# The Units stage of a dilated-attention layer: VectorE, ScalarE and GpSimd ordered by hand beside TensorE, with rope, mixes, weight pairs and loads cut into steps over several slots

## The chip, the cores and the metric

The kernel runs on one core of one Trainium2 chip. The metric is the device time of one execution in microseconds (us), the median of several runs; lower is better. A core has engines with a queue of instructions each: TensorE (PE, with its weight loads as PEld), VectorE (DVE), ScalarE (ACT), GpSimd (POOL) and SyncE (SP), which here only issues DMAs. An engine goes through its queue in order; an instruction whose data isn't there holds up those behind it.

## The reference

Two pre-norm residual layers on 2048 tokens of width 1024: the first with gated linear attention, the second with dilated sliding-window attention in three groups of heads (window and dilation 128/1, 512/4, 2048/16; six heads of width 128 in each); each layer also has a small attention into a memory, a SiLU gate and an output projection. The change touches the second layer's mixer:

```
def dilated_mixer(h, w_in):
    for g, (window, dil) in enumerate(DIL_GROUPS):
        qkv = (h @ w_in[:, base:base + 3 * MIXER_WIDTH]).reshape(B, T, 3, DIL_HEADS, DIL_HEAD_DIM)
        q = partial_rope(qkv[:, :, 0], pos)          # rotates 32 of the 128 columns
        k = partial_rope(qkv[:, :, 1], pos)
        o, lse = dilated_group(q, k, qkv[:, :, 2], window, dil)
    wts = jax.nn.softmax(jnp.stack(lses, axis=0), axis=0)
    o = jnp.einsum('gbth,gbthd->bthd', wts, jnp.stack(outs, axis=0).astype(jnp.float32))
```

So the three groups' outputs of one head number are mixed with weights from the groups' log-sum-exps: a mix needs all three.

## The kernel before, in words

Products are made in three 16-bit matmuls (`mm3`, L180 to L182: high by high, high by low, low by high), so each operand exists as a high and a low half. The Units stage takes up the second layer's heads: 18 heads, in triples of groups 2, 1, 0, eight slots each, 144 slots s. In slot s, PE does the scores of step s - 10 (`att_scores`), the values of step s - 13 (`att_pv`), and one projection `proj_t` of 24 matmuls (q on even slots, k on odd ones, 512 tokens each). PE's order is written out by hand (`manual_schedule` at L1157); DVE, ACT, POOL and SP get theirs from a scheduler, which places the instructions by when it reckons them ready.

What the other engines do for one slot:

- scores: DVE adds the mask and takes the maximum (L1234, into pm and mx), makes the bias st (L1238); ACT takes the exponential with its row sum (L1243); `split_P` cuts pm into the high half (L173, ACT) and the low half (L174, POOL), and SP transposes both by DMA (L175, ph to pt). The values' matmuls three slots later read pt. Every second step DVE copies the output bank (L1272, osb) and SP stores it (L1274).
- `evac`, after each pair of projections: ACT copies 32 rows for the rotation into rx (L1182) and writes the high half (L1185), DVE the low half (L1186).
- `rope_quad`, once per four slots: DVE swaps (L1192), POOL multiplies by one table (L1193), DVE by the other (L1194), DVE adds (L1195), ACT makes the high half (L1198), DVE the low half (L1199), and eight DVE copies (L1204) put them into q and k. There is one rx and one rw buffer. The scores of a head begin two slots after its last projection and need these copies.
- weights of the next head: SP loads them (L807), ACT squares (L816), PE sums over partitions (L825, into a bank of ps_tr, of which there are two; values and statistics use them as well), ACT takes logarithm and exponential (L827, L828), and `pair_split` makes halves (L839 ACT, L840 DVE).
- v: one DMA of 1 MB per head (L1176).

After the last head of a triple comes its mix. At x = 0 of the counter x = (s - 35) mod 24, `att_stats` transposes the statistics on PE (L1283), copies (L1286) and stores them; `prep_load` and `prep_mix` work out the weights and store them to DRAM (fd). Then four items, one per 512 tokens: `item_og` loads the gate sg and the three outputs og, `item_fb` loads the weights onto all partitions (L1343, fb), `item_mix` multiplies on POOL (L1350, L1355) and DVE (L1352), adds (L1358, L1359), multiplies by the gate (L1361) and stores (L1363, brd). og, fb and sg have one buffer each. The program puts the items four slots apart (two for the last triple); where each engine does them is the scheduler's choice. Behind the stage comes a tail: the last triple's rest, the gate's projection, the output projection and the final norm.

Of the kernel before, what the change touches and what calls it, by code (L numbers as in the profile page):

```python
# [16 lines left out]
P = 128  # L17
T = 2048
D = 1024
KT = 8  # L20
# [10 lines left out]
GROUPS = ((1, 16), (4, 4), (16, 1))  # L31
SUMS_AT = (6, 8, 10, 12, 13, 14)
# [3 lines left out]
def trunk(ctx, tc, a, out):  # L36
# [765 lines left out]
    def pair_raw(c0s):  # L802
        raw = tl(stg, [P, KT, 256], F32, "stg")
        for j, c0 in enumerate(c0s):
            v = w_in_b[:, c0:c0 + P].rearrange("(k p) n -> p k n", p=P)
            for k0 in (0, 4):
                SY.dma_start(raw[:, k0:k0 + 4, j * P:(j + 1) * P], v[:, k0:k0 + 4, :])  # L807
        return dict(raw=raw, w=[], m=len(c0s))

    def pair_norm(d, cps, common=False):  # L810
        raw = d["raw"]
        m = d["m"]
        d["w"] = [tl(wp, [P, 2, KT, P], F16, "w") for _ in range(m)]
        rm = tl(sp, [P, 2], F32, "rm")
        for j in range(m):
            A.activation(out=d["w"][j][:, 1].bitcast(BF16), in_=raw[:, :, j * P:(j + 1) * P], func=AF.Square,  # L816
                         accum_out=rm[:, j:j + 1])
        n = 1 if common else m
        rb = tl(sp, [P, n], BF16, f"rb{n}")
        if common:  # L820
            V.tensor_tensor(out=rb, in0=rm[:, 0:1], in1=rm[:, 1:2], op=ALU.add)
        else:
            V.tensor_copy(rb, rm[:, 0:n])
        tot = bank(cps)[:, 0:n]
        PE.matmul(tot, ones, rb, start=True, stop=True)  # L825
        s = tl(sp, [P, n], F32, f"ws{n}")
        A.activation(out=s, in_=tot, func=AF.Ln, bias=tiny)  # L827
        A.activation(out=s, in_=s, func=AF.Exp, scale=-0.5, bias=lscale)  # L828
# [7 lines left out]

    def pair_split(d, j):
        w, r = d["w"][j], d["raw"][:, :, j * P:(j + 1) * P]
        A.activation(out=w[:, 0], in_=r, func=AF.Copy, scale=d["s"][j])  # L839
        V.scalar_tensor_tensor(out=w[:, 1], in0=r, scalar=d["s"][j], in1=w[:, 0], op0=ALU.mult, op1=ALU.subtract)  # L840
# [338 lines left out]
    def evac(ts, c, g, dsts, X):  # L1179
        r0 = 64 * (c // 2)  # L1180
        for j in range(2):
            A.activation(out=X[r0 + 32 * j:r0 + 32 * j + 32, :], in_=ts[j][0:32, :], func=AF.Copy)  # L1182
        for j in range(2):
            hi = gdst(dsts[j][:, 0, :], g, c)
            A.activation(out=hi, in_=perm(ts[j], g), func=AF.Copy, scale=SQ)  # L1185
            V.scalar_tensor_tensor(out=gdst(dsts[j][:, 1, :], g, c), in0=perm(ts[j], g), scalar=SQ, in1=hi,  # L1186
                                   op0=ALU.mult, op1=ALU.subtract)

    def rope_quad(c, g, dsts, X):
# [4 lines left out]
        V.tensor_tensor(out=X, in0=X, in1=rope[0][:, cs], op=ALU.mult)  # L1194
        V.tensor_tensor(out=W, in0=X, in1=W, op=ALU.add)  # L1195
        hl = X.bitcast(F16).rearrange("p (a n) -> p a n", a=2)
        hi, lo = fold(hl[:, 0], g), fold(hl[:, 1], g)
        A.activation(out=hi, in_=perm(W, g), func=AF.Copy, scale=SQ)  # L1198
# [7 lines left out]
    def att_scores(hd, step):  # L1206
# [31 lines left out]
        V.tensor_scalar(out=st[:, jc:jc + 2], in0=mx, scalar1=nsc, scalar2=LSP, op0=ALU.mult, op1=ALU.add)  # L1238
        at = 0
# [136 lines left out]
    def scores(at):  # L1376
        att_scores(hds[at // 8], at % 8)

    def pv(at):
        att_pv(hds[at // 8], at % 8)  # L1380
        if at % 8 == 7 and at // 8 % 3 < 2:
            att_stats(hds.pop(at // 8), 0)

    preps, items = {}, {}
    for s in range(NS):
        n, e = divmod(s, 8)
        if s >= 10:
            scores(s - 10)
# [273 lines left out]
```

## Time and profile before

| what | value |
| --- | --- |
| median of 3 runs | 2650.81 us (2650.23 to 2655.42) |
| profiled execution | 2649.36 us |
| its span, first to last instruction | 2647.6 us |
| PE busy | 2515.3 us (95%), 17033 matmuls |
| DVE busy | 1602.7 us (61%) |
| ACT busy | 1341.2 us (51%) |
| POOL busy | 566.8 us (21%) |
| scores of slot 10 to scores of slot 144 | 1498.71 to 2402.02 us |

How to read it: matmul ends are modelled, so "busy" for PE says that it had work and not that it ran at its best; the granted clock stands beside it (1.00 is full). In a row of a timeline stand the start, the length, the engine and the line, what is written and read, and in brackets the idle time of the engine before it with what ended it. Rows of groups give the count, busy time, the mean in ns, and idle time before. The program's names leave the buffer numbers out: q, k, rx, rw, pm, ph, pt, fb as above.

### The profile page before, as it was taken

How to read it: one execution, taken by the hardware profiler on the slowest of the kernel's cores; microseconds unless marked ns; L12 is line 12 of the kernel's file. 1: busy time of each engine (PE TensorE's matmuls, PEld its weight loads, DVE VectorE, ACT ScalarE, POOL GpSimd, SP SyncE). 2: the span in 40 equal slices, each digit the busy share in tenths (PEclk: the TensorE clock that was granted, in tenths of full speed). 3: DMA queues.
4: the chain of work that ended last, by engine and by line, in shares of the span. 5: the costliest groups of instructions: out<-in, count | busy, mean ns of one | idle time of the engine just before them, and what ended most of it. 6: DMA issues, size and time to landing. Idle time of an engine off the chain costs nothing.

```text
span 2647.6 us, 45024 instructions
## 1 busy us (share of the span) xinstructions
PE 2515.3 (95%) x17033; PEld 1686.3 (64%) x17033; DVE 1602.7 (61%) x3582; ACT 1341.2 (51%) x2944; POOL 566.8 (21%) x471
## 2 busy tenths in 40 slices
PE   7999999899999899999999999999899998988899
PEld 6879999788889644444444455455454454545798
DVE  7445544666866756656545555776757667577742
ACT  7355444544444446656536455455464554646322
POOL 0000000011211224545541122322323223222200
PEclk9999999899999999999999999999899999999899
DMA  6232111444543645677664144564636647358642
GB/s 207 83 128 97 63 57 71 124 122 120 154 128 106 193 132 141 169 163 190 161 177 149 53 91 101 151 159 110 179 97 154 156 108 181 98 153 222 189 162 87
DMA packets 555533, 356.53 MB, mean 135 GB/s; under 512 B 382690, under 2 KB 494772, under 8 KB 552628
## 3 DMA queue, kind: packets, MB, share of 16 engines
q1 hardware_dynamic: 555316, 353.66, 48.8%
q8 instruction: 133, 2.18, 0.3%
q14 instruction: 84, 0.69, 0.1%
HBM read 185.74 MB, written 95.86 MB: 106 GB/s over the span
## 4 chain that ended last, share of the span: by engine, by line
PE 72%; DMA 8%; DVE 8%; issue 4%; ACT 4%; POOL 2%; SPq 1%; DVEq 0%; ACTq 0%; POOLq 0%
PE ps_mm L180 14%; PE ps_mm L181 14%; PE ps_mm L182 14%; PE ps_x L180 5%; PE ps_x L181 5%; PE ps_x L182 5%; DMA pt<-ph 2%; DMA fb<-fd 2%; PE ps_o L180 1%; PE ps_o L182 1%; PE ps_o L181 1%; DMA mpt<-stg 1%; PE ps_tr L167 1%; DMA stg<-in_w_in_b 1%; PE ps_g L181 1%
## 5 line engine op out<-in xcount | busy, mean ns | idle before, releaser
L180 PE MATMUL ps_mm<-h2T,w 128*128 128x512 f16 x1112 | 428.6, 385 | 5.9 <-ACT w L839 4.7
L182 PE MATMUL ps_mm<-h2T,w 128*128 128x512 f16 x1112 | 427.0, 384 | 0.7 <-DVE w L840 0.7
L181 PE MATMUL ps_mm<-h2T,w 128*128 128x512 f16 x1112 | 427.7, 385 | 0.0
L180 PE MATMUL ps_mm<-w,hT 128*128 128x256 f16 (+1 forms) x1408 | 389.0, 276 | 3.3 <-ACT v L490 1.3
L181 PE MATMUL ps_mm<-w,hT 128*128 128x256 f16 (+1 forms) x1408 | 388.0, 276 | 0.0
L182 PE MATMUL ps_mm<-w,hT 128*128 128x256 f16 (+1 forms) x1408 | 386.6, 276 | 0.4 <-DVE hT L384 0.4
L182 PEld LDWEIGHTS <-w 128*128 128x128 f16 x1952 | 192.5, 99 | 236.5 <-issue 8.7
L180 PEld LDWEIGHTS <-w 128*128 128x128 f16 x1952 | 192.8, 99 | 219.7 <-issue 8.0
L181 PEld LDWEIGHTS <-w 128*128 128x128 f16 x1952 | 192.6, 99 | 219.8 <-issue 13.9
L174 POOL TENSOR_TENSOR ph<-pm,ph 128x512 f16<-128x512 f32 (+2 forms) x144 | 147.4, 1024 | 613.2 <-ACT ph L173 446.1
L1243 ACT ACTIVATE pm<-pm,st,cols 128x256 f32<-128x256 f32 (+1 forms) x288 | 156.4, 544 | 171.2 <-DVE st L1238 169.2
L180 PE MATMUL ps_x<-h2T,w 128*128 128x512 f16 x552 | 209.2, 379 | 1.3 <-DVE c L1059 1.3
L182 PE MATMUL ps_x<-h2T,w 128*128 128x512 f16 x552 | 209.2, 379 | 0.0
L181 PE MATMUL ps_x<-h2T,w 128*128 128x512 f16 x552 | 209.2, 379 | 0.0
L174 POOL TENSOR_TENSOR stg<-mp,stg 128x512 f16<-128x512 f32 x16 | 18.6, 1160 | 746.3 <-DMA ogd<-og 456.6
L180 PEld LDWEIGHTS <-hT 128*128 128x128 f16 x1408 | 139.4, 99 | 24.7 <-issue 5.4
L181 PEld LDWEIGHTS <-hT 128*128 128x128 f16 x1408 | 139.3, 99 | 23.5 <-issue 4.5
L1234 DVE CUSTOM_DVE_ANT_0 pm<-ps_g,mw 128x256 f32<-128x256 f32 (+1 forms) x288 | 93.5, 360 | 96.3 <-PE ps_g L182 95.2
L182 PEld LDWEIGHTS <-hT 128*128 128x128 f16 x1408 | 139.9, 99 | 18.5 <-DVE hT L384 0.7
L1182 ACT ACTIVATE rx<-ps_mm 32x512 f32<-32x512 f32 x96 | 56.2, 585 | 136.5 <-DVE k L1204 64.7
L181 PE MATMUL ps_g<-k,q 128*128 128x256 f16 (+1 forms) x288 | 70.3, 253 | 16.2 <-DVE k L1204 16.2
L180 PE MATMUL ps_g<-k,q 128*128 128x256 f16 (+1 forms) x288 | 68.6, 251 | 15.6 <-DVE k L1204 15.6
(502 smaller groups left out, 6015.0 us busy)
## 6 DMA issues: line engine op xcount, KB each, us to landing
stg<-in_w_in_b SPq DMA_DIRECT2D x80, 256.0 KB
v<-vd SPq DMA_DIRECT2D x18, 1024.0 KB
fb<-fd SPq DMA_DIRECT2D x24, 768.0 KB
od<-osb SPq DMA_DIRECT2D x68, 256.0 KB
og<-od SPq DMA_DIRECT2D x68, 256.0 KB
x<-in_x SPq DMA_DIRECT2D x32, 512.0 KB
stg<-in_w_in_b SPq DMA_DIRECT2D x24, 512.0 KB
vd<-vo SPq DMA_DIRECT2D x48, 256.0 KB
```

The source lines that it names most:

```text
L167: PE.transpose(t[:, (k - k0) * P:(k - k0 + 1) * P], src[:, k * P:(k + 1) * P], ident)
L174: G.tensor_tensor(out=lo, in0=src, in1=hi, op=ALU.subtract)
L180: PE.matmul(o, sh, mh, start=first, stop=False)
L181: PE.matmul(o, sh, ml, start=False, stop=False)
L182: PE.matmul(o, sl, mh, start=False, stop=last)
L1182: A.activation(out=X[r0 + 32 * j:r0 + 32 * j + 32, :], in_=ts[j][0:32, :], func=AF.Copy)
L1234: V.tensor_tensor_reduce(out=pm[:, at:at + w * P], in0=s[:, at:at + w * P], in1=masks["mw" if w == 2 else "mf"], scale=1.0, scalar=NEG, op ...
L1243: A.activation(out=p_, in_=p_, func=AF.Exp, scale=sc, bias=st[:, jc + jj:jc + jj + 1], accum_out=st[:, ns + jc + jj:ns + jc + jj + 1])
```

## The change

In the Units stage, DVE, ACT and POOL are now ordered by hand as well (`MANUAL`); SP is not. Their order is that of the new program text, slot by slot:

- scores: masks, st, then `evac` of the projection before (as `mid`), then the exponentials and the split;
- rope, in slots 0 and 4 of each head: `rope_a` (swap and both products) behind the scores of the slot, `rope_b` (sum, high half) behind the values, `rope_c` (low half, copies) behind the projection;
- weight pairs: load, square (slot 2), sum (slot 3, `pair_sum`; before in slot 2), scaling and halves in slots 4 to 6 (`later` puts a step into a later slot);
- v: four DMAs of a quarter each, in slots 4 to 7, instead of one in slot 6;
- mixes: statistics at x = 0 with their copy and store a slot later (`stats_out`), load, softmax and output of the weights at x = 1, 2 and 3, `item_mul` at x = 7, 11, 15, 19 and `item_sum` a slot later, the loads of the next item in the slot of the sum. The last triple's items stand three slots apart, and two of its sums fall into the tail.

```
+MANUAL = ("PE", "DVE", "Activation", "Pool")
...
-    def load_v(n):
+    def load_v(n, x):
         u, i = heads[n]
-        vt = tl(vp, [P, 4, 2, 4, P], F16, "v")
-        SY.dma_start(vt, v_d[u[0], u[1], i])
-        return vt
+        if x == 0:
+            hds[n]["v"] = tl(vp, [P, 4, 2, 4, P], F16, "v")
+        SY.dma_start(hds[n]["v"][:, x], v_d[u[0], u[1], i][:, x])
...
+    def mixes(s):
+        h, x = divmod(s - 35, 24)
+        if not 0 <= h < 5:
+            if s < NS:
+                return
+            h, x = 4, s - 131
+        step = 4 if h < 4 else 3
+        if x == 0:
+            later(s + 1, stats_out, *att_stats(hds[3 * h + 2], 0))
+        if x == 1:
+            preps[h] = prep_load(h)
+        if x == 2:
+            preps[h] = prep_mix(preps[h])
+        if x == 3:
+            prep_out(*preps.pop(h))
+        if h == 4:
+            x += 1
+        for y in range(4):
+            if x == 7 + step * y:
+                item_mul(*items[y])
+            if x == 8 + step * y:
+                item_sum(*items.pop(y))
+        for y in range(4):
+            if x == 8 + step * (y - 1):
+                items[y] = (item_og(h, y), item_fb(h, y))
...
+    with ExitStack() as c5:
+        c5.enter_context(tc.manual_schedule(engines={getattr(mybir.EngineType, e_) for e_ in MANUAL}))
+        chunk = None
+        for s in range(NS):
+            n, e = divmod(s, 8)
+
+            def mid():
+                if chunk:
+                    evac(*chunk)
+
+            if s >= 10:
+                scores(s - 10, mid)
+            else:
+                mid()
+            if s % 4 == 0 and s > 0:
+                pn, pc = (s - 1) // 8, (s // 4 - 1) % 2
+                pg, pq = heads[pn][0][1], hds[pn]["qk"]
+                W = rope_a(pc, rx)
+            if s >= 13:
+                pv(s - 13)
+            if s % 4 == 0 and s > 0:
+                rope_b(pg, rx, W)
...
+            c = (0, 2, 1, 3)[e // 2]
+            t = proj_t(d["w"][e % 2], c)
+            if s % 4 == 0 and s > 0:
+                rope_c(pc, pg, pq, rx, W)
+            if e % 4 == 0:
+                rx = tl(bk, [P, 512], F32, "rx")
+            chunk = (t, e % 2, c, u[1], hds[n]["qk"][e % 2], rx)
+            for f in todo.pop(s, []):
+                f()
+            m = wnext["m"]
+            if n > 0 and e < m:
+                pair_load(wnext, e)
+            if e == 2:
+                pair_sq(wnext)
+            if e == 3:
+                pair_sum(wnext, ps_tr)
+                later(s + 1, pair_scale, wnext)
+                later(s + 1, pair_hi, wnext, 0)
+                later(s + 2, pair_lo, wnext, 0)
...
+            if e > 3:
+                load_v(n, e - 4)
+            mixes(s)
             wcur = wnext
```

GpSimd's queue where the first mixes begin, from the subtraction of about slot 38 on; ph is the split of a slot, rw the rope product, fb the products of an item. Before:

```order
L174 TENSOR_TENSOR ph_18519<-pm_18507,ph_18519 128x256
L1350 TENSOR_TENSOR fb_18646<-og_18642,fb_18646 128x512
L1355 TENSOR_TENSOR fb_18646<-og_18642,fb_18646 128x512
L1193 TENSOR_TENSOR rw_18562<-rw_18562,rope_2301_16246 128x512
L174 TENSOR_TENSOR ph_18591<-pm_18579,ph_18591 128x256
L1350 TENSOR_TENSOR fb_18921<-og_18917,fb_18921 128x512
L1355 TENSOR_TENSOR fb_18921<-og_18917,fb_18921 128x512
L174 TENSOR_TENSOR ph_18662<-pm_18650,ph_18662 128x256
L174 TENSOR_TENSOR ph_18720<-pm_18708,ph_18720 128x384
L1350 TENSOR_TENSOR fb_19197<-og_19193,fb_19197 128x512
L1355 TENSOR_TENSOR fb_19197<-og_19193,fb_19197 128x512
```

and in the changed program (L175 is the subtraction, L1211 rope's product, L1384 and L1389 an item's products):

```order
L175 TENSOR_TENSOR ph_18680<-pm_18665,ph_18680 128x256
L175 TENSOR_TENSOR ph_18737<-pm_18722,ph_18737 128x384
L1384 TENSOR_TENSOR fb_18582<-og_18578,fb_18582 128x512
L1389 TENSOR_TENSOR fb_18582<-og_18578,fb_18582 128x512
L175 TENSOR_TENSOR ph_18801<-pm_18786,ph_18801 128x512
L175 TENSOR_TENSOR ph_18874<-pm_18859,ph_18874 128x384
L1211 TENSOR_TENSOR rw_18879<-rw_18879,rope_2301_16246 128x512
L175 TENSOR_TENSOR ph_18958<-pm_18943,ph_18958 128x512
L175 TENSOR_TENSOR ph_19018<-pm_19003,ph_19018 128x384
L1384 TENSOR_TENSOR fb_18855<-og_18851,fb_18855 128x512
L1389 TENSOR_TENSOR fb_18855<-og_18851,fb_18855 128x512
```

Three items stood within some four slots; now there are four slots between one item and the next, and rope's product stands two slots from either.

VectorE's queue in a rope slot (slot 24): masks (ISA), st, the low half of k, the copy of the output bank, and rope's steps. Before:

```order
L1234 ISA pm_17495,mx_17494<-ps_g_17493,mw_16243 128x256
L1234 ISA mx_17494 128x1
L1192 STREAM_SHUFFLE rw_17478<-rx_17295 128x512
L1186 SCALAR_TENSOR_TENSOR k_17006<-ps_x_17447,k_17006 128x512
L1238 TENSOR_SCALAR st_2397_17095<-mx_17494,cols_88 128x2
L1272 COPY osb_17521<-ps_tr_17437 128x512
L1194 TENSOR_TENSOR rx_17295<-rx_17295,rope_2300_16245 128x512
L1195 TENSOR_TENSOR rw_17478<-rx_17295,rw_17478 128x512
L1199 SCALAR_TENSOR_TENSOR rx_17295<-rw_17478,rx_17295 128x512
```

and now:

```order
L1257 ISA pm_17488,mx_17487<-ps_g_17486,mw_16243 128x256
L1257 ISA mx_17487 128x1
L1261 TENSOR_SCALAR st_2397_17100<-mx_17487,cols_88 128x2
L1204 SCALAR_TENSOR_TENSOR k_17005<-ps_x_17460,k_17005 128x512
L1210 STREAM_SHUFFLE rw_17508<-rx_17297 128x512
L1212 TENSOR_TENSOR rx_17297<-rx_17297,rope_2300_16245 128x512
L1297 COPY osb_17521<-ps_tr_17450 128x512
L1216 TENSOR_TENSOR rw_17508<-rx_17297,rw_17508 128x512
L1481 TENSOR_SCALAR cols_88<-cols_88 128x1
L315 TENSOR_SCALAR cols_88<-cols_88 128x1
L1222 SCALAR_TENSOR_TENSOR rx_17297<-rw_17508,rx_17297 128x512
```

The bias st, on which the exponentials wait, now stands directly behind the masks; the swap, rope's first step, stands behind st and the low half.

TensorE's queue at the end of slot 35, where the first triple's statistics are transposed (L1283, now L1308). Before:

```order
L181 MATMUL ps_x_18259<-h2T_5115,w_17677 128x512
L182 LDWEIGHTS w_17677
L182 MATMUL ps_x_18259<-h2T_5115,w_17677 128x512
L1283 MATMUL ps_tr_18305<-ident_82,st_2470_17619 32x128
L180 LDWEIGHTS q_17526
```

and now:

```order
L183 MATMUL ps_x_18266<-h2T_5115,w_17688 128x512
L830 LDWEIGHTS ones_86
L830 MATMUL ps_tr_18293<-rb_2561_18291,ones_86 128x2
L1308 MATMUL ps_tr_18298<-ident_82,st_2470_17627 32x128
L181 LDWEIGHTS q_17528
```

The weights' sum (L830), a slot earlier before, now stands directly ahead of the transpose, and both write a bank of ps_tr.

More of the change, by code (lines that the diff above doesn't have):

```diff
@@ L800, in wbase, with pair_raw @@
         return u[1] * 2304 + u[0] * 256
[L802 to L818, printed above, removed]
+    def pair_raw(c0s, now=True):
+        d = dict(raw=tl(stg, [P, KT, 256], F32, "stg"), w=[], m=len(c0s), c0=c0s)
+        if now:
+            for j in range(d["m"]):
+                pair_load(d, j)
+        return d
@@ new lines, in pair_load, with pair_sq @@
+    def pair_load(d, j):
+        v = w_in_b[:, d["c0"][j]:d["c0"][j] + P].rearrange("(k p) n -> p k n", p=P)
+        for k0 in (0, 4):
+            SY.dma_start(d["raw"][:, k0:k0 + 4, j * P:(j + 1) * P], v[:, k0:k0 + 4, :])
+    def pair_sq(d):
+        d["w"] = [tl(wp, [P, 2, KT, P], F16, "w") for _ in range(d["m"])]
+        d["rm"] = tl(sp, [P, 2], F32, "rm")
+        for j in range(d["m"]):
+            A.activation(out=d["w"][j][:, 1].bitcast(BF16), in_=d["raw"][:, :, j * P:(j + 1) * P], func=AF.Square,
+                         accum_out=d["rm"][:, j:j + 1])
@@ L1171, in trunk, with evac, rope_a @@
     qp = c4.enter_context(pool("qp", 2))
-    def load_v(n):
+    def load_v(n, x):
         u, i = heads[n]
-        vt = tl(vp, [P, 4, 2, 4, P], F16, "v")
-        SY.dma_start(vt, v_d[u[0], u[1], i])
-        return vt
[L1179 to L1189, printed above, removed]
+        if x == 0:
+            hds[n]["v"] = tl(vp, [P, 4, 2, 4, P], F16, "v")
+        SY.dma_start(hds[n]["v"][:, x], v_d[u[0], u[1], i][:, x])
+    def evac(t, j, c, g, dst, X):
+        r0 = 64 * (c // 2) + 32 * j
+        A.activation(out=X[r0:r0 + 32, :], in_=t[0:32, :], func=AF.Copy)
+        hi = gdst(dst[:, 0, :], g, c)
+        A.activation(out=hi, in_=perm(t, g), func=AF.Copy, scale=SQ)
+        V.scalar_tensor_tensor(out=gdst(dst[:, 1, :], g, c), in0=perm(t, g), scalar=SQ, in1=hi, op0=ALU.mult,
+                               op1=ALU.subtract)
+    def rope_a(c, X):
         cs = slice(c * 512, (c + 1) * 512)
@@ L1204, in rope_quad, with att_scores @@
                     V.tensor_copy(gdst(dsts[j][0:32, x, :], g, c + 2 * y), fold(hl[r0:r0 + 32, x], g))
-    def att_scores(hd, step):
+    def att_scores(hd, step, mid=None):
         u = hd["u"]
@@ L1469, in trunk @@
             pv(NS - 13 + x)
+        if x == 4:
+            stats_out(*att_stats(hds.pop(NH - 2), 0))
+        if x < 4:
+            for f in todo.pop(NS + x, []):
+                f()
+            mixes(NS + x)
         if x == 7:
@@ L1477, in trunk @@
         if 0 <= c < 4 and not odd:
-            att_stats(last, c)
+            stats_out(*att_stats(last, c))
         c, odd = divmod(x - 4, 2)
@@ L1492, in trunk @@
         if 0 <= c < 4 and not odd:
-            sg = item_mix(its.pop(c), fbs.pop(c), last["osb"].pop(c))
+            it = its.pop(c), fbs.pop(c), last["osb"].pop(c)
+            item_mul(*it)
+            sg = item_sum(*it)
             b5s[c] = tl(vp, [P, 2, 512], F32R, "v")
```

122 lines of the change are left out of this document (63 added, 59 removed).

## The prediction

> **What bounds the kernel now.** I read the page first, then the busy time by stretches, then PE's waits in the Units stage, then the timelines around two of those waits.
>
> ```profile
> span 2647.6 us, 45024 instructions
> ```
>
> The profiled execution took 2649.36 us: the span and 1.76 us around it. The median of the runs is 2650.81, 1.45 above that. The Units stage has 144 slots; a slot is one projection, one step of scores and one of values. A triple of heads (one head of each group) is 24 slots and repeats. I cut the stretches at scores of slots 18, 42, 66, 90, 114, 138 and 144, and slots 18 to 23 apart. Columns: length, busy time of PE, PEld, DVE, ACT and POOL, PE's granted clock, DMA share, GB/s.
>
> ```profile
> 1544.53:1581.87 37.34, 37.34 (x229) 19.98 (x228) 19.38 (x61) 23.25 (x54) 6.98 (x7) 1.00 0.59 119
> 1544.53:1694.09 149.56, 149.56 (x919) 80.31 (x918) 91.31 (x262) 83.87 (x194) 34.46 (x31) 1.00 0.49 115
> 1694.09:1856.39 162.30, 152.94 (x920) 81.38 (x918) 113.36 (x290) 87.14 (x200) 44.22 (x38) 0.98 0.53 141
> 1856.39:2022.52 166.13, 154.62 (x919) 82.10 (x918) 112.68 (x289) 86.46 (x198) 44.77 (x38) 0.96 0.54 138
> 2022.52:2187.09 164.57, 153.93 (x920) 81.60 (x918) 112.96 (x290) 87.18 (x200) 44.21 (x38) 0.97 0.55 140
> 2187.09:2351.70 164.61, 153.27 (x920) 81.69 (x919) 111.73 (x287) 85.32 (x195) 44.38 (x38) 0.97 0.54 136
> 2351.70:2402.02 50.32, 40.81 (x228) 20.90 (x227) 40.83 (x89) 23.61 (x54) 16.99 (x13) 0.90 0.75 199
> 2402.02:2647.60 245.58, 222.98 (x1455) 191.84 (x1453) 125.01 (x242) 84.65 (x200) 29.83 (x21) 0.95 0.54 159
> ```
>
> PE is the bound: in the second row, a triple before any mix, it is busy for all of the 149.56 us, at clock 1.00. So what can be won is PE's idle time and its slow clock. The next four do the same matmuls beside the mixes of the triple before, and take 162.30 + 166.13 + 164.57 + 164.61 = 657.61, against 4 x 149.56 = 598.24: 59.37 too much. The short stretch takes 50.32 where the same slots of a clean triple take 37.34: 12.98. So the mixes cost the stage 72.35 us. DVE has only 113 us of work in 162: the trouble is when things come, not how much. PE's waits from 1370 to 2460 name it (total, times, longest):
>
> ```profile
> PE ps_o L180 <- DMA pt<-ph: 21.7, 6, 5.5
> PE ps_g L181 <- DVE k L1204: 16.2, 5, 3.5
> PE ps_g L180 <- DVE k L1204: 15.6, 5, 4.2
> PE ps_tr L1283 <- ACT pm L1243: 8.7, 2, 6.1
> PE ps_tr L180 <- DMA pt<-ph: 1.7, 1, 1.7
> ```
>
> Together 63.9 us; the two waits at L1283 lie in the tail, and so does one for pt, 2.82 us:
>
> ```profile
> 2455.15 0.29 PE L180 MATMUL ps_o<-pt,v 128*128 128x128 f16 x1 [2.82 <-DMA pt<-ph]
> ```
>
> That leaves 63.9 - 8.7 - 2.8 = 52.4 us of gaps in the Units stage; the other 20 of the 72.35 are matmuls at a granted clock under 1. One us of gap thus cost 72.35 / 52.4 = 1.38 us.
>
> The first kind of wait, on the timelines of DVE, ACT, POOL and PE around slot 42:
>
> ```profile
> 1683.77 1.02 DVE L1352 TENSOR_TENSOR fb<-og,fb 128x512 f32<-128x512 f32 x1 [2.94 <-DMA fb<-fd]
> 1692.85 0.49 ACT L1243 ACTIVATE pm<-pm,st,cols 128x128 f32<-128x128 f32 x1 [9.05 <-DVE st L1238]
> 1698.75 1.56 POOL L1355 TENSOR_TENSOR fb<-og,fb 128x512 f32<-128x512 f32 x1
> 1698.95 1.50 DVE L1204 COPY k<-rx 32x512 f16<-32x512 f16 x1
> 1696.99 0.27 PE L180 MATMUL ps_g<-k,q 128*128 128x256 f16 x1 [2.56 <-DVE k L1204]
> 1700.50 0.37 PE L181 MATMUL ps_g<-k,q 128*128 128x256 f16 x1 [3.25 <-DVE k L1204]
> ```
>
> DVE stands 2.94 us for fb in front of the masks; ACT gets its exponentials 9.05 us late, rope's ACT step stands behind them, and the copies L1204 into q and k are the last thing that PE's scores need. The second kind, around slot 46, on DVE, SP and the chain:
>
> ```profile
> 1719.91 1.94 DVE L1361 TENSOR_TENSOR sg<-fb,sg 128x512 f32<-128x512 f32 x1
> 1721.88 0.56 SPq L1363 DMA_DIRECT2D brd<-sg  x1
> 1723.66 8.28 DMA pt<-ph
> 1731.99 0.22 PE L180 MATMUL ps_o<-pt,v 128*128 128x128 f16 x1 [3.55 <-DMA pt<-ph]
> ```
>
> L1361 is late, SP's store of it heads its queue, and v, fb and the transpose of ph follow in one lump; the transpose then takes 8.28 us and PE waits for pt.
>
> **The change part by part.** No work is added, only order: 20 items of five instructions stay 20 items, 33 ropes stay 33.
>
> Mixes spread. In the order of before, the GpSimd multiplications of a triple's four items come out within some six slots; now one item stands every four slots, its sums a slot behind its products, its loads three slots ahead. What a load needs:
>
> ```profile
> 1708.44 0.43 SPq L1343 DMA_DIRECT2D fb<-fd  x1
> 1713.32 1.02 DVE L1352 TENSOR_TENSOR fb<-og,fb 128x512 f32<-128x512 f32 x1 [2.53 <-DMA fb<-fd]
> ```
>
> That is 4.9 us from issue to use, against three slots of about 6.2 (149.56 / 24), 18.7 us. Even with 8.28 us more, as for the transpose above, it lands in time. So DVE no longer waits there: both kinds of wait lose their start, -72.35. What hides the items then is DVE's free time: a triple has 113.36 us for DVE, 113.36 - 91.31 = 22 of them for the mixes, 5.5 an item, and a clean triple's 149.56 leaves 36 free. If that cover were gone, the lag would go to the masks and from there to rope.
>
> Rope by hand. Of the three steps the second and third now sit strictly behind the slot's own scores work, and the GpSimd product behind the slot's subtraction L174. A clean case of before, slot 32: its first scores, DVE's last copy, and the scores that need it two slots on.
>
> ```profile
> 1633.18 0.27 PE L180 MATMUL ps_g<-k,q 128*128 128x256 f16 x1
> 1643.66 0.28 DVE L1204 COPY k<-rx 32x512 f16<-32x512 f16 x1
> 1646.18 0.22 PE L180 MATMUL ps_g<-k,q 128*128 128x128 f16 x1
> ```
>
> The copies end 10.76 us after the slot's start, PE asks at 13.0: 2.24 us to spare. For the new chain I add the groups (line, shape, count | busy, mean ns):
>
> ```profile
> L1234 DVE CUSTOM_DVE_ANT_0 pm<-ps_g,mw 128x256 f32<-128x256 f32 x142 | 55.8, 420 | 38.4 <-PE ps_g L182 37.7
> L1243 ACT ACTIVATE pm<-pm,st,cols 128x256 f32<-128x256 f32 x141 | 83.0, 589 | 33.2 <-DVE st L1238 32.8
> L1243 ACT ACTIVATION_READ_ACCUMULATOR pm<-pm,st,cols 128x1 f32 x264 | 49.3, 187 | 0.0
> L173 ACT ACTIVATE ph<-pm 128x512 f16<-128x512 f32 x57 | 35.7, 626 | 1.4
> L174 POOL TENSOR_TENSOR ph<-pm,ph 128x512 f16<-128x512 f32 x57 | 70.0, 1229 | 281.2 <-ACT ph L173 191.2 <-issue 75.5 <-DMA v<-vd 14.4
> L1193 POOL TENSOR_TENSOR rw<-rw,rope 128x512 f32<-128x512 f32 x33 | 41.8, 1267 | 51.0 <-DVE rw L1192 51.0
> L1195 DVE TENSOR_TENSOR rw<-rx,rw 128x512 f32<-128x512 f32 x33 | 24.5, 743 | 2.4
> L1198 ACT ACTIVATE rx<-rw 128x512 f16<-128x512 f32 x33 | 30.6, 928 | 9.0 <-DVE rw L1195 9.0
> L1199 DVE SCALAR_TENSOR_TENSOR rx<-rw,rx 128x512 f16<-128x512 f32 x33 | 32.4, 982 | 42.1 <-ACT rx L1198 42.1
> ```
>
> Scores of six matmuls 0.7, masks 2 x 0.42, the small st 0.3, exponentials 2 x 0.78, L173 0.63, subtraction 1.23, rope's product 1.27, sum 0.74, high half 0.93, low half 0.98, eight copies 8 x 0.28 = 2.24: 11.4, and some 0.05 of handoff at each of ten steps, 11.9 us. That is a us later than before and still 1.1 us ahead of PE, so I take 0. Bounds: 11.4 and, with the copies at the 1.50 of the row above, 11.9 + 8 x 1.22 = 21.7. The upper end is far: in the new order no GpSimd instruction stands beside the copies, because GpSimd's next subtraction needs masks that DVE does behind them. I add 1 us in all for heads that start with DVE behind.
>
> That copy of 1.50 us ran beside GpSimd's L1355 and the uncontended ones take 0.28. [...]
>
> Pair sums a slot later. In slots 35, 59, 83, 107 and 131 the small matmul of the weights' norm now stands directly ahead of the transpose of the statistics, which needs one of two ps_tr buffers, held by this matmul and the values. PE then waits for ACT's read:
>
> ```profile
> L827 ACT ACTIVATE ws<-ps_tr,cols 128x2 f32<-128x2 f32 x16 | 4.2, 262 | 0.4
> ```
>
> 0.26 and two handoffs, 0.5 us, five times: +2.5. Bounds: 0, if the values' buffer is free already, and +7, if ACT is in a pair of exponentials (0.78) and reads after it. Nothing covers this; PE goes in order.
>
> Loads spread. On SP, which isn't ordered by hand, the four v loads still come out in a row, ahead of a transpose. With DVE in time, the transpose needs 8.28 us in the worst lump, while PE asks three slots later, 18.7 us: 0.
>
> The tail. Its 245.58 us hold 8.7 + 2.8 us of waits. Two of the last triple's mixes now fall into its first slots, which speaks against, and the masks there no longer stand behind a lump of mixes, which speaks for. I take 0, between -6 (the longer wait at L1283 goes) and +6 (it comes twice).
>
> Sum: 2647.6 - 72.35 + 1 + 2.5 + 0 = 2578.8 of span; + 1.76 = 2580.5 for the profiled execution, + 1.45 = 2582 for the median.
>
> The gap of 3.55 us at 1731.99 and those of 2.56 and 3.25 decide the price of what is left. [...] These rows don't tell lone gaps from gaps that follow each other closely, so they leave it open.
>
> **The rivals.**
>
> First, the transposes stay late: v, fb and og still stand ahead of pt in SP's order, and that was half of the gaps. pt's waits in the Units stage, 21.7 + 1.7 - 2.8 = 20.6 us, remain at 1.0 to 1.38: 2582 + 21 to 28 = 2603 to 2610. For it speaks the unchanged SP order, against it that those lumps formed behind a late L1361. Chance 0.10.
>
> Second, rope comes a little late: if the chain takes 14 to 15 us instead of 11.9, PE waits 1 to 2 us in each of 17 heads, 17 x 1.5 x 1.0 to 1.38 = 26 to 35: 2608 to 2617. For it: the strict order takes away the scheduler's freedom, and the spare falls from 2.24 to 1.1. Chance 0.12.
>
> Third, slower: DVE falls behind in the rope slot. Masks, st and sums stand in one line there, and each is as late as its slowest neighbour. The gain of 68.9 us is spent when each of 17 heads waits 68.9 / 17 / 1.38 = 2.9 us, that is when the copies end at 13.0 + 2.9 = 15.9 us, 4 later than I add up. At 6 later: 17 x 4.9 x 1.38 = 115, 2697. Against it: the clean case at 10.76 and DVE's 36 us free. Chance 0.05, a fifth of it near no change.
>
> Fourth, no change: the mixes' 72 us are paid elsewhere, in slots 24 to 41, at the same total. Chance 0.01.
>
> **How the numbers follow.** The forecast has 0.72, with 2573 to 2592 as its own range (-6 - 2.5 below, +6 + 4.5 above). For eight in ten the range goes on to the first rival and to most of the second: 2570 to 2614. No change means within 0.2%, 5.3 us, about what a measurement of this kernel can tell. Faster 0.72 + 0.10 + 0.12 = 0.94, same 0.01 + 0.01 = 0.02, slower 0.04.
>
> **What would show it.** Right: stretches of 24 slots at 150 to 152 us with clock 1.00; no wait for k or pt in the slots; L1352's successor without idle time for fb; copies' end 11.9 us after their slot's start; 0.5 us ahead of five transposes. Wrong: waits of PE for k or q at every eighth slot (second or third rival), or for pt four slots after (first).

## The result and the profile after

| what | before | after |
| --- | --- | --- |
| median | 2651.78 us (4 runs, 2650.23 to 2655.42) | 2590.39 us (4 runs, 2588.60 to 2593.54) |
| ratio | | 0.9768, 95% interval 0.9751 to 0.9785 |
| profiled execution, span | 2649.36, 2647.6 us | 2593.54, 2591.8 us |
| slot 18 to slot 144 of the Units stage | 857.49 us | 788.34 us |
| tail, slot 144 to the end | 245.58 us | 259.19 us |

The change is faster by 2.3%, inside the range of 2570 to 2614 and 8.4 us above the forecast of 2582. The Units stage gained 69.15 us, and the tail gave back 13.61.

The busy time by stretches of the changed kernel, cut at the scores of slots 18, 42, 66, 90, 138 and 144 (columns as before; of the lines in what follows, L1227 was L1204 before, L1204 was L1186, L1257 was L1234, L1268 was L1243, L1308 was L1283 and L1386 was L1352):

```profile
1544.27:1694.37 150.10, 149.72 (x919) 80.25 (x918) 86.06 (x263) 86.55 (x197) 33.03 (x30) 1.00 0.43 108
1694.37:1844.59 150.22, 149.84 (x920) 80.26 (x918) 108.28 (x291) 87.77 (x199) 47.72 (x38) 1.00 0.61 151
1844.59:1995.07 150.48, 149.88 (x920) 80.24 (x918) 108.94 (x292) 87.90 (x199) 47.37 (x38) 1.00 0.59 156
...
2295.27:2332.61 37.34, 37.34 (x229) 19.98 (x228) 28.60 (x70) 20.17 (x48) 13.17 (x11) 1.00 0.76 174
2332.61:2591.80 259.19, 224.34 (x1455) 191.64 (x1453) 137.70 (x256) 87.03 (x202) 37.21 (x24) 0.94 0.58 167
```

A triple beside mixes now takes 150.1 to 150.5 us where it took 162 to 166, the six slots that took 50.32 take 37.34, and the clock is 1.00 in all of them. DVE's busy time hardly fell (113 to 108 us): the same work comes at other times. In the last row PE has as much to do as before (224 against 223 us), in a stretch that is 13.6 us longer.

PE's waits from 1370 to 2460:

```profile
PE ps_tr L1308 <- ACT pm L1268: 12.6, 3, 11.3
PE ps_mm L181 <- DVE x L1651: 8.5, 1, 8.5
PE ps_tr L181 <- DMA pt<-ph: 6.3, 5, 2.4
PE ps_tr L1308 <- ACT ws L832: 1.9, 5, 0.4
PE ps_o L181 <- DMA pt<-ph: 1.1, 2, 0.9
```

The waits for the rope copies (31.8 us before) are gone, and all but the fourth row lie in the tail, save one wait of 0.2 us for pt. The fourth is the new wait at the statistics, five times 0.38 us. What DVE waits for between slots 18 and 144, in full:

```profile
DVE pm L1257 <- PE ps_g L183: 89.0, 35, 5.2
DVE rw L1216 <- POOL rw L1211: 47.5, 31, 2.0
DVE k L1204 <- ACT k L1203: 38.4, 33, 1.8
DVE rx L1222 <- ACT rx L1217: 26.2, 31, 1.2
DVE q L1204 <- ACT q L1203: 17.3, 29, 0.8
DVE mn L1341 <- DMA nm<-std: 2.5, 3, 1.2
```

The first row is DVE in time, waiting for scores. The row that stood here before is missing now. Its ten waits stand in slots 40 and 43, 64 and 67 and so on, two in each triple, each some slots ahead of one of the ten places where TensorE stalled:

```profile
DVE fb L1352 <- DMA fb<-fd: 32.5, 10, 4.1
```

### The profile page after: what moved, and what is told of

It reads as the page before. It is cut to its first block, busy times and chain, and to the rows that moved or that the text cites. A ratio compares the mean times of both kernels' runs of the same rounds, so it can differ in the third digit from the quotient of the medians.

```text
span 2591.8 us, 45023 instructions
## 1 busy us (share of the span) xinstructions
PE 2497.6 (96%) x17033; PEld 1678.4 (65%) x17033; DVE 1576.0 (61%) x3582; ACT 1345.9 (52%) x2944; POOL 582.6 (22%) x471
## 5 line engine op out<-in xcount | busy, mean ns | idle before, releaser
L181 PE MATMUL ps_mm<-h2T,w 128*128 128x512 f16 x1112 | 422.7, 380 | 7.0 <-ACT w L851 5.7
L183 PE MATMUL ps_mm<-h2T,w 128*128 128x512 f16 x1112 | 422.4, 380 | 0.3 <-DVE w L855 0.3
L182 PE MATMUL ps_mm<-h2T,w 128*128 128x512 f16 x1112 | 422.5, 380 | 0.0
L175 POOL TENSOR_TENSOR ph<-pm,ph 128x512 f16<-128x512 f32 (+2 forms) x144 | 165.8, 1151 | 638.2 <-ACT ph L174 441.5
L1268 ACT ACTIVATE pm<-pm,st,cols 128x256 f32<-128x256 f32 (+1 forms) x288 | 156.2, 544 | 79.8 <-DVE st L1261 78.2
L175 POOL TENSOR_TENSOR stg<-mp,stg 128x512 f16<-128x512 f32 x16 | 18.6, 1160 | 743.7 <-DMA ogd<-og 456.9
L1257 DVE CUSTOM_DVE_ANT_0 pm<-ps_g,mw 128x256 f32<-128x256 f32 (+1 forms) x288 | 93.0, 359 | 103.8 <-PE ps_g L183 103.0
L1217 ACT ACTIVATE rx<-rw 128x512 f16<-128x512 f32 x36 | 33.9, 941 | 115.7 <-DVE rw L1216 115.7
L174 ACT ACTIVATE ph<-pm 128x512 f16<-128x512 f32 (+2 forms) x144 | 77.2, 536 | 4.5
```

Source lines behind the costliest of these rows:

```text
L174: A.activation(out=hi, in_=src, func=AF.Copy)
L175: G.tensor_tensor(out=lo, in0=src, in1=hi, op=ALU.subtract)
L181: PE.matmul(o, sh, mh, start=first, stop=False)
L182: PE.matmul(o, sh, ml, start=False, stop=False)
L183: PE.matmul(o, sl, mh, start=False, stop=last)
L1217: A.activation(out=fold(X.bitcast(F16)[:, 0:512], g), in_=perm(W, g), func=AF.Copy, scale=SQ)
```

## The experiments

Two things came together in the change: an order by hand for DVE, ACT and POOL, and a text cut into steps that stand in chosen slots. The first question was which of them brings the gain; the second, what the other pieces are worth; the third, where the tail's 13.6 us come from. In what follows "Units" is slot 18 to slot 144 of the profiled execution, 857.5 us before and 788.3 after, and "tail" the rest, 245.6 and 259.2.

### Mixes in a lump again

```
-            if x == 7 + step * y:
+            if x == (7 + y if h < 4 else 7 + step * y):
                 item_mul(*items[y])
-            if x == 8 + step * y:
+                if h < 4:
+                    item_sum(*items.pop(y))
+            if h == 4 and x == 8 + step * y:
                 item_sum(*items.pop(y))
...
-            if x == 8 + step * (y - 1):
+            if x == (6 + y if h < 4 else 8 + step * (y - 1)):
                 items[y] = (item_og(h, y), item_fb(h, y))
```

> The changed kernel with the four items of a triple put one slot apart again (products and sums of an item in the same slot, x = 7 to 10, its loads one slot ahead); the rest by hand as it is. Theory A (the gain is that the mixes are spread, so that their loads land before VectorE comes to them): an item takes about 5 us of loads plus 3.1 us of products plus 3 us of sums in a slot of 6.2, so the lag grows by some 5 us per item to 15 or 20 us, and waits of TensorE for pt or for the rope copies return in the four full triples: 30 to 70 us slower than the changed kernel (2620 to 2660). Rival B (the order by hand of the three engines, with rope in steps, brings the gain): within 5 us of the changed kernel.

2666.89 us (2665.56 to 2668.91), ratio to the kernel before 1.0059 (1.0044 to 1.0074): 76.5 us above the changed kernel, a little over theory A's range and far from B's. Units took 867.3 us. PE's waits, the first and the third row, and DVE at the second item of the first lump (its wait for fb, and the sum that needs GpSimd's product):

```profile
PE ps_g L181 <- DVE mx L1257: 41.6, 8, 8.0
...
PE ps_tr L830 <- DVE rb L828: 7.9, 4, 2.5
```

```profile
1709.94 1.02 DVE L1386 TENSOR_TENSOR fb<-og,fb 128x512 f32<-128x512 f32 x1 [5.11 <-DMA fb<-fd]
1712.08 1.99 DVE L1396 TENSOR_TENSOR fb<-fb 128x512 f32<-128x512 f32 x1 [1.12 <-POOL fb L1384]
```

DVE stands 5.11 us for fb, as before the change, and the masks queue behind it until PE has no free bank for scores (mx). It isn't pt and the copies that PE waits for this time, but the masks themselves: the same start, another end.

### The lump two slots earlier

The same with 5 + y for 7 + y and 4 + y for 6 + y, beside the rope that slot 42 needs.

> As the run before, but with the four items at x = 5 to 8 (slots 40 to 43), beside the rope that the scores of slot 42 need, about where the scheduler of the kernel before had put them. Theory A: waits for the rope copies at slot 42 and for pt some slots later come back as in the kernel before: 40 to 75 us slower than the changed kernel (2630 to 2665), and slower than the lump two slots later. Rival B: within 5 us of the changed kernel.

2690.52 us (2683.24 to 2692.06), ratio 1.0142 (1.0127 to 1.0158), 100 us above the changed kernel and 24 above the other lump, so worse in this place, as theory A had it, and by more than it had. Units 890.7 us. Nearly all of PE's waits in the Units stage are one row, and it isn't the wait for the copies that theory A named (6.4 us in all):

```profile
PE ps_tr L830 <- DVE rb L828: 79.8, 4, 21.4
```

Four waits of 20 us: the operand of the weights' sum (rb) is cast on DVE, in order, behind four items. What PE needs of a late DVE is whatever stands next in the order.

### The text of before, ordered as it stands

```
+    with ExitStack() as c5:
+        c5.enter_context(tc.manual_schedule(engines={getattr(mybir.EngineType, e_) for e_ in MANUAL}))
     for s in range(NS):
```

> The kernel before, its program text unchanged, with VectorE, ScalarE and GpSimd ordered as that text stands (four slots between items, loads two slots ahead, rope as one block, weight pairs as one block, loads in one piece). Theory A: the order alone keeps the items apart, so most of the gain is there without any cutting into steps: the Units stage within 0 to 15 us of the changed kernel's, and the tail (no mixes fall into it here) near the 245.6 us of before: 2572 to 2600. Rival B (the cutting into steps over slots is needed, since rope as a block holds VectorE through the masks): TensorE waits in most heads, at least 30 us slower than the changed kernel, over 2620.

2823.67 us (2815.64 to 2824.92), ratio 1.0644 (1.0628 to 1.066): 172 us slower than before. Theory A expected most of the gain here, and that was wrong; rival B's "at least 30 us" holds with much to spare. The items are apart and DVE no longer stands for fb, but Units takes 1020 us. PE's first three waits:

```profile
PE ps_tr L826 <- DVE rb L824: 83.2, 17, 9.8
PE ps_mm L181 <- DVE q L1187: 49.7, 18, 3.5
PE ps_g L181 <- DVE mx L1235: 28.4, 17, 3.4
```

17 or 18 times each, so once per head and not once per triple. What DVE itself waits for most, in the stage:

```profile
DVE q L1187 <- ACT q L1186: 263.8, 63, 8.4
```

In that text the evacuation stands directly behind its own projection, so DVE comes to it early, stands 4.2 us each time for ACT's high half, and has rope, the weights and the next slot's masks behind it. The changed text puts it a slot later, behind masks that are due. So an order by hand loses on the old text and gains on the new one. That the evacuation's place is the main reason is argued from these rows and not shown: no run moved the evacuation alone.

### The steps, ordered by the scheduler

```
-MANUAL = ("PE", "DVE", "Activation", "Pool")
+MANUAL = ("PE",)
```

> The changed program text, cut into steps as it is, with the order by hand taken back for VectorE, ScalarE and GpSimd (only TensorE's order stays by hand). Theory A1 (the scheduler's placing of the items in a lump is what cost the kernel before its 72 us, and only an order by hand prevents it): the items stand in a lump again, the waits for pt and rope copies return: 2630 to 2660, near the kernel before. Rival B1 (the cutting of the text into steps already keeps things apart): 2580 to 2600.

2675.38 us (2673.40 to 2677.70), ratio 1.0076 (1.0058 to 1.0093). Units 883.3 us, tail 246.0. Theory A1 holds in its main point, though the time is above its range of 2630 to 2660: the items stand in a lump again on POOL, and the waits for fb and for the rope copies are back. DVE's row for fb (the largest in DVE's list is another, 83.2 us of rope's swap waiting for ACT), then PE's first three rows:

```profile
DVE fb L1386 <- DMA fb<-fd: 51.5, 16, 6.1
```

```profile
PE ps_tr L1308 <- ACT ws L832: 38.8, 10, 8.9
PE ps_g L182 <- DVE k L1227: 22.7, 5, 5.7
PE ps_g L181 <- DVE k L1227: 10.2, 5, 3.8
```

The first of PE's rows is new against the kernel before, and more than the 25.8 us by which Units is longer. Five of its waits, 0.96 us each, stand in the five slots of the prediction. The other five, 5.8 to 8.9 us, stand in slots 44, 68, 92, 116 and 140, where the statistics of another head are transposed a slot after the sum, and ACT, late, hasn't read the sum's bank yet. So the sum's later place, priced at 0.5 us, costs up to 8.9 with ACT late; no run took it back under the scheduler. Thus neither half of the change pays alone: 172 us lost with the order without the steps, 20 with the steps without the order (each against its own runs of the kernel before), 61 gained with both.

### One step undone at a time

Weight pairs as one block (`pair_norm` in slot 2, `pair_split` of a block of columns in slots 4 and 5):

```
-            if e == 2:
-                pair_sq(wnext)
-            if e == 3:
-                pair_sum(wnext, ps_tr)
...
+            if e == 2:
+                pair_norm(wnext, ps_tr)
+            if 4 <= e < 4 + m:
+                pair_split(wnext, e - 4)
```

> The changed kernel with only the steps of the weight pairs undone: squares, sum and scaling as one block at the end of slot 2, halves of a column block together in slots 4 and 5. In the text-ordered run TensorE waited 83 us in 17 places for the sum's operand. Theory A2 (that was because the block's later instructions hold VectorE and ScalarE in front of the next slot's masks, whatever else is there): 40 to 90 us slower than the changed kernel, 2630 to 2680, with waits at the sum's matmul. Rival B2 (adding up the rows: the squares end 6.3 us after the slot's start, the sum's turn comes at 6.2, so the block costs 0.3 to 1 us in 17 places, and the 83 us came from VectorE being late for other reasons): 5 to 17 us slower, 2595 to 2608.

2606.51 us (2605.09 to 2607.08), ratio 0.9815 (0.9799 to 0.9832), 16 us above the changed kernel: rival B2, at the upper end of its range, and not the 40 to 90 of A2. Units 804.9 us. The wait in full, one of its places, the clock behind that place, and the stage (columns as before):

```profile
PE ps_tr L830 <- DVE rb L828: 16.4, 9, 2.3
```

```profile
2010.36 0.16 PE L830 MATMUL ps_tr<-rb,ones 128*128 128x2 bf16 x1 [2.23 <-DVE rb L828]
```

```profile
2010.30:2013.71 3.41, 3.35 (x17) 2.13 (x17) 2.46 (x8) 1.74 (x4) 1.45 (x1) 0.50 0.25 57
```

```profile
1545.25:2350.17 804.92, 788.44 (x4818) 422.15 (x4817) 540.03 (x1499) 465.97 (x1048) 220.70 (x193) 1.00 0.58 143
```

Nine places with 1.3 to 2.25 us each and not 17 with 0.3 to 1. So of the text order's 83 us for rb, some 16 would be the block's own; the rest then came from DVE being late.

Rope as one block directly behind the scores (`rope_b` and `rope_c` moved up to `rope_a`):

> The changed kernel with rope's three steps in one block directly behind the scores of its slot. Theory A3 (the cutting of rope is needed too: VectorE stands some 4 us for GpSimd and ScalarE in every fourth slot, and copies and masks come late): 10 to 40 us slower, 2600 to 2630. Rival B3 (the chain of rope is as long either way, 11 to 12 us against TensorE's 13.0, and only the copy of the output bank moves behind it, whose bank is needed four slots later): within 4 us of the changed kernel.

2595.27 us (2590.69 to 2595.76), ratio 0.9769 (0.9748 to 0.9791) beside 0.9768 for the change: no difference that can be measured, as rival B3 said. (By the medians it is 4.9 us, but the kernel before, run beside it, had 2654.87 and not 2651.78.) Units 790.3 us, 2 more. With the rest in place, cutting rope is worth nothing that can be measured.

The loads as before (v in one DMA in slot 6, a pair's four in slot 0):

> The changed kernel with its loads as before: v in one DMA of 1 MB in slot 6, a weight pair's four DMAs together in slot 0. Theory A (the loads' place is worth nothing as long as VectorE is in time, since TensorE asks for pt three slots later): within 4 us of the changed kernel. Rival (pieces keep the transposes of ph short): waits for pt return, 10 to 25 us slower, 2600 to 2615.

2591.70 us (2588.57 to 2593.57), ratio 0.9759 (0.9741 to 0.9776), Units 788.3 us: theory A, no difference. "Loads spread" is no part of the gain.

The sum into a bank of the scores:

```
-                pair_sum(wnext, ps_tr)
+                pair_sum(wnext, ps_g)
```

> The changed kernel with one word changed: the weights' sum goes to a bank of the scores (ps_g) instead of ps_tr, so that the transpose of the statistics, directly behind it in TensorE's order, finds a free bank. By the term of the prediction (0.5 us in five places) and the five waits of 0.38 us in the changed kernel's trace (slots of 6.85 us against 6.28): 2 to 3 us faster than the changed kernel, the slots 35, 59, 83, 107 and 131 at 6.28 us. Rival (the transpose waits for the values' bank anyway, or the sum now makes the scores wait): within 1 us, slots unchanged or the wait at the scores of slots 36 and after.

The wait of the transpose for ACT's read (1.9 us, five times) is gone, and slots 35, 59, 83, 107 and 131 take 6.31 us. Units 786.3 us, 2.0 less, as the term said. The median is 2589.18 (2586.36 to 2592.43), ratio 0.9761 (0.9741 to 0.9780): 1.2 us lower, which the runs don't resolve.

### The tail

What begins it in the changed kernel, on DVE and PE (items of the last triple, then of the last head):

```profile
2357.72 1.02 DVE L1386 TENSOR_TENSOR fb<-og,fb 128x512 f32<-128x512 f32 x1 [2.76 <-DMA fb<-fd]
2358.66 0.28 DVE L1257 CUSTOM_DVE_ANT_0 pm<-ps_g,mw 128x128 f32<-128x128 f32 x1
...
2425.66 1.01 DVE L1386 TENSOR_TENSOR fb<-rw,fb 128x512 f32<-128x512 f32 x1 [8.14 <-DMA fb<-fd]
...
2430.87 0.67 DVE L1651 TENSOR_TENSOR x<-ps_mm,x 128x512 f32<-128x512 f32 x1
```

```profile
2367.41 0.38 PE L1308 MATMUL ps_tr<-ident,st 128*8 128x128 f32 x1 [11.33 <-ACT pm L1268]
```

```profile
2431.59 0.79 PE L181 MATMUL ps_mm<-wh,q 128*128 128x512 f32 x1 [8.50 <-DVE x L1651]
```

Twice DVE stands for an item's fb with something behind it that PE needs: masks at 2357, the addition of x at 2425. The transpose waits 11.33 us (6.05 before), the output projection 8.50 (4.49 before, behind a wait of DVE for fb of 5.17 us):

```profile
2488.23 0.80 PE L180 MATMUL ps_mm<-wh,q 128*128 128x512 f32 x1 [4.49 <-DVE x L1556]
```

So only the wait at 2357 is new; the one at x is longer than it was. Counted from the scores of slot 144, those of slot 148 begin after 26.6 us before and 35.0 now, those of slot 152 after 47.4 and 58.4, the output projection after 86.2 and 99.0. Of the 13.6 us, 11 are thus lost by slot 152, ahead of the wait at x. My theory was that the first of the two waits is to blame: two mixes of the last triple spill into the tail. Four runs tried it.

The last triple's items two slots apart, none in the tail (step 2 instead of 3, products and sum in one slot):

> The changed kernel with the last triple's items two slots apart, products and sums in the same slot, so that all four are done before slot 144 and none falls into the tail. Theory A (the tail's 13.6 us over before come from the mixes that spill into it: VectorE stands 2.8 us for fb and does two items in front of the masks on which the transpose of the statistics waits): 7 to 14 us faster than the changed kernel, 2576 to 2584, the wait of the transpose down from 11.3 to about 6 us. Rival B (the tail is slower because rope's last part, the weights' halves and the scheduler's own order changed, not by the spilled mixes): within 3 us of the changed kernel.

2588.25 us (2584.91 to 2594.98), ratio 0.9758 (0.9742 to 0.9774), 2 us lower, within the scatter. The tail is 250.9 us, 8.3 less, and the transpose's longest wait 4.9, as theory A said; but the 7 to 14 us that it expected in all did not come. Units is 7.2 us more: with items two slots apart, slots 139, 140 and 143 are 1.7 to 2.6 us longer, the first of them behind a wait for DVE's rb. About the same 8 us are paid on the other side of the cut.

The spilled items' arithmetic left out:

```
             if x == 7 + step * y:
-                item_mul(*items[y])
+                if h < 4 or y < 2:
+                    item_mul(*items[y])
             if x == 8 + step * y:
-                item_sum(*items.pop(y))
+                if h < 4 or y < 2:
+                    item_sum(*items.pop(y))
+                else:
+                    (h_, c_, sg, og), fb = items.pop(y)
+                    SY.dma_start(br_d[c_][:, :, h_, :], sg.rearrange("p (n t) -> p n t", n=4))
```

> The changed kernel without the arithmetic of the last triple's items 2 and 3 (slots 143 to 147): their loads and the store of the unmixed gate stay, the products and sums are left out, so this part of the output is not the mix. Theory A (the tail is 13.6 us longer because these two items stand on VectorE and GpSimd ahead of the masks of slots 145 to 147): tail 245 to 251 us instead of 259, the longest wait of the transpose 6 us or less, 8 to 14 us faster than the changed kernel, 2576 to 2582. Rival B (VectorE is late there for rope's last part, the weights' halves and the gate alone): tail within 4 us of 259, 2586 to 2594.

2590.57 us (2584.35 to 2592.82), ratio 0.9761 (0.9739 to 0.9782): no faster. Slot 147, which holds the transpose's wait, falls from 17.45 to 9.38 us, but slot 146 grows from 4.13 to 7.45: slot 148 begins 29.5 us after slot 144, 5.5 earlier than in the changed kernel. The tail is 253.3, 5.9 less and still 7.7 above before, with the second wait longer than it was:

```profile
PE ps_mm L181 <- DVE x L1656: 10.1, 1, 10.1
PE ps_tr L181 <- DMA pt<-ph: 5.7, 3, 3.7
PE ps_tr L1308 <- ACT pm L1268: 5.3, 1, 5.3
```

The expectation of A (2576 to 2582) failed. By these two profiles the spilled arithmetic is worth 5.9 of the 13.6 us; the medians show none of it. What stays is the chain from the last head's scores to x: statistics, their store, weights, fb of the second item. From the scores of slot 152 to the output projection it takes 38.8 us before, 40.6 in the changed kernel and 41.3 here; DMAs of 5.53 us (statistics), 1.97 (weights) and 7.09 (fb) are part of it in the changed kernel.

The order by hand through the tail's first four slots, the masks ahead of the spilled item (and the sum in ps_g):

```
+        if x == 4:
+            c6.close()
         if x < 10:
-            scores(NS - 10 + x)
+            scores(NS - 10 + x, (lambda: evac(*chunk)) if x == 0 else None)
+        if x == 0:
+            W = rope_a(1, rx)
...
-            gate_silu(gt.pop(c), c)
+            gq.append(gate_a(gt.pop(c), c))
```

> The changed kernel with the weights' sum in a bank of the scores (ps_g) instead of ps_tr, and the order by hand kept up through the first four slots of the tail, with rope's last part cut as in the stage and the gate's SiLU in two steps, so that the masks of slots 146 and 147 stand ahead of the spilled mix. Theory A (the transpose of the tail waits 11.3 us because the scheduler put the spilled mix, which stands 2.8 us for fb, ahead of the masks): the wait falls to 6 us or less, the five waits of 0.4 us at the statistics go; 8 to 16 us faster than the changed kernel, 2575 to 2583. Rival B (VectorE has simply too much work in those slots, whatever the order): the tail within 4 us, only the 2 to 3 us of the five waits gained, 2586 to 2590.

2589.03 us (2588.53 to 2594.95), ratio 0.9767 (0.974 to 0.9793). The transpose still waits 10.9 us; Units 786.0, tail 257.2: the numbers of rival B. But in this order DVE stands for another thing in front of the masks, ACT's half of the output weights (L1535 was L1526):

```profile
2353.33 1.22 DVE L1535 TENSOR_TENSOR w<-stg,w 128x1024 fp32r<-128x1024 f32 x1 [3.10 <-ACT w L1534]
2354.47 0.28 DVE L1257 CUSTOM_DVE_ANT_0 pm<-ps_g,mw 128x128 f32<-128x128 f32 x1
```

One wait took the place of the other, so the run shows that this order is no better, and not that none is. The next run also puts the last head's items later in the text (`prep_mix` of the second ahead of the first item, items 2 and 3 in the output projection's loop):

> As the run before, and the last head's items later in the text: the second prep ahead of the first item, items 2 and 3 in the output projection's loop. Theory A' (TensorE's wait of 8.5 us for the addition of x is VectorE standing 8.1 us for the fb of the second item, which is loaded late since prep and item stand in that order): that wait falls to 0 to 4 us, 4 to 10 us faster than the run before. Rival B' (the chain from the statistics to fb is as long either way, or the scheduler puts the items early again): within 3 us of the run before.

2589.38 us (2588.96 to 2594.18), ratio 0.9769 (0.9739 to 0.98). The wait at x is 5.5 us beside 4.7 in the run before: rival B'. No version tried beats the changed kernel by what a run can tell.

Tails of all profiles side by side: with the spilled items on hand-ordered engines 259.2, 256.9, 254.0, 255.3, 253.1, 255.7, 257.2, 257.7 and 252.3 us (after, the two lumps, loads, pair, rope, the two tails, sum); without the spill 245.6 (before), 249.1 (text order), 250.9 (two slots apart), 253.3 (left out); steps under the scheduler 246.0. The first group's median is 255.7, so some 10 us above before is what the change costs there by the profiles; 259.2 is the group's top. The medians of all executions put it at 7.8 (69.15 gained in Units, 61.39 in all), if Units is the same in every execution. And the spill is only part of it: without it, but with the Units stage ordered by hand, the tail is still 3.5 to 7.7 us above before, in one profile each.

## Why the prediction was right, and where it was off

**The Units stage.** The three terms were -72.35, +1 and +2.5, together -68.9 us; measured -69.15. By parts:

- Mixes spread, -72.35. The clean triples' sum for slot 18 to 144 is 5 x 149.56 + 37.34 = 785.14 us; the changed kernel takes 788.34, so all but 3.2 us of the excess went. That the items' place does it is shown: with all else as it is, a lump brings back 76 or 100 us. That spreading pays only with the rest of the text changed too is what the prediction didn't see: it treated the order by hand as the means to put the items apart and looked at its cost in rope alone, while the text order run shows 172 us of it in weights, evacuations and masks.
- Rope by hand, 0, and +1 for heads that start late. In the changed kernel, slot 32 on PE and DVE (each x2 row holds two copies):

```profile
1632.92 0.27 PE L181 MATMUL ps_g<-k,q 128*128 128x256 f16 x1
1645.91 0.22 PE L181 MATMUL ps_g<-k,q 128*128 128x128 f16 x1
```

```profile
1639.40 0.69 DVE L1216 TENSOR_TENSOR rw<-rx,rw 128x512 f32<-128x512 f32 x1 [2.01 <-POOL rw L1211]
1643.64 0.49 DVE L1227 COPY k<-rx 32x512 f16<-32x512 f16 x2
```

The copies end 11.2 us after the slot's start, where the sum over rows gave 11.9, and PE asks at 13.0. The wait for GpSimd's product (2.01 us) is there, and hidden. In slot 40 nothing is to spare:

```profile
1682.67 0.22 PE L181 MATMUL ps_g<-k,q 128*128 128x128 f16 x1
...
1694.37 0.22 PE L181 MATMUL ps_g<-k,q 128*128 128x128 f16 x1
```

```profile
1695.25 0.49 DVE L1227 COPY k<-rx 32x512 f16<-32x512 f16 x2
```

The last copies end 13.1 us after the start and PE asks at 11.7; it lost only 0.12 us, since its first steps didn't wait for those last copies. The term of 1 us came out as at most 0.3: slots 42 and 66 took 6.13 and 6.39 us, against 6.01 for 90 and 114, and 0.22 of slot 66 is the wait for pt. The bound of 21.7 us for colliding copies was never near: they take 0.28 us in all ropes, 248 copies with no GpSimd product beside them.

```profile
L1227 DVE COPY k<-rx 32x512 f16<-32x512 f16 x124 | 30.1, 279 | 0.8
L1227 DVE COPY q<-rx 32x512 f16<-32x512 f16 x124 | 29.6, 275 | 0.5
```

Before, the mean was 0.38 to 0.40 us: of 248 copies between slots 18 and 144, 35 ran beside a GpSimd instruction and took 1.06 us in the mean, the other 213 took 0.28.

- Pair sums, +2.5. Five places, each slot 6.85 us against 6.28: 2.9. The mechanism was right:

```profile
1658.27 0.17 PE L830 MATMUL ps_tr<-rb,ones 128*128 128x2 bf16 x1
1658.82 0.28 PE L1308 MATMUL ps_tr<-ident,st 128*32 128x128 f32 x1 [0.38 <-ACT ws L832]
```

- Loads, 0: measured 0.

**The tail.** This is the step that failed: "I take 0, between -6 and +6". In the profiled execution it was +13.6, in the group of nine about +10. The prediction named the spilled mixes and set against them the masks that "no longer stand behind a lump". It priced one wait alone, the longer one at the transpose. PE's waits in the tail grew in three places: for the transposes from 8.7 to 12.6 us, for pt from 2.8 to 7.2, and for x from 4.5 to 8.5, together 12.3 of the 13.6. The wait of 4.49 us for x stood in the tail of before as well, at 2488.23; the prediction's 8.7 + 2.8 us leave it out, since its view ended at 2460. What it also left out: a wait of DVE for fb moves into the tail, ahead of masks, and behind it stands a chain of DMAs (statistics to fb) of about 40 us from the last head's scores to x, so that what is lost by slot 152 isn't won back. The run without the spilled arithmetic begins slot 148 5.5 us earlier and has a tail 5.9 shorter. What the rest is, isn't settled; moving the order within the tail changed the time by less than can be measured.

**The sum.** 2578.8 of span were forecast, 2591.8 measured, and the 13.0 are the tail. The profiled execution was the slowest of the four: the median is 3.15 us below it, where the forecast added 1.45; that takes 4.6 off the error and leaves 8.4.

**The rivals.** Transposes late: no. On SP the four quarters of v still stand in a row ahead of a transpose (issued from 1712.00 on, the transpose at 1714.75), and with DVE in time PE waits for pt once in the Units stage, 0.2 us; the load run says the same. Rope late, DVE behind: not in the change; but they are what the text order and the lumps show, at 76 to 233 us above the change, where the prediction priced them at 26 to 115. What keeps them away is DVE in time in every slot, and that took the order and the changed text together. Undone one at a time, rope's steps were worth 2 us of Units, the loads nothing and the pairs' steps 16.6, where the text order is 231.8 above the change; the evacuation's later place was not undone alone. The prediction gave 0.05 to it on the ground that DVE has 36 us free in a triple. The text order's DVE has as much free time and still loses 172 us, so free time was a weak reason.

**The price of a gap.** I took 1.38 us for each us of gap. In the run with weight pairs as a block, PE's idle time is 804.92 - 788.44 = 16.5 us, nearly all of it in nine gaps of 1.3 to 2.25 us, and Units is 19.8 us above the clean sum of 785.14: price 1.2. Behind one of the nine, of 2.23 us, the clock was at 0.50 for 3.41 us; behind the others it stayed at 1.00. In the kernel before the price was 1.38, with gaps of 2.6 and 3.3 us close behind each other. My factor was too high for these short gaps that stand alone, and a factor of 1, the lower end of the rivals' prices, would have been too low. It entered only the rivals' prices.

Two counts of the prediction are off and touch no sum: an item has six instructions, two on GpSimd and four on VectorE, and there are 36 ropes, of which the window of its rows held 33.

## What to carry to other kernels

When stalls stand at two places of a period and the stretches between run clean, sum the excess against a clean period: that bound (72.35) was also the gain, to 5%. Before ordering engines by hand, look in the text for instructions that come to their turn before their operands do, with work behind them that TensorE needs, and move those to a later place; order and changed text were worth something only together. Not every cut pays: that of rope was worth 2 us, that of the weight pairs 16.6. And look at where the period ends: work that is spread over time spills past the end, where nothing may cover it.

## What was not expected of the hardware

A short gap slowed the clock in some places and not in others. Take the gaps of PE in all Units stages here that have no other of over 0.2 us within 8 us. Of nine gaps of 1.27 to 1.77 us none was followed by the clock at 0.50 (within 3.5 us of its end), of ten of 1.87 to 2.78 us five were, and of 38 of 3.25 us and more 36 were. In the kernel before, that of 3.55 us ahead of 1731.99 was not, and those of 4.17, 5.10 and 5.46 us were. And the tail differs by 7 us between profiles of kernels whose text is the same there (252.3 to 259.2 us), with the wait for x anywhere from 1.5 to 8.5 us, while the Units stage takes 788.34 and 788.28 us in the change and in the load run.
